# Binding the matmul order of the first four Strassen units of an FFN, with one more split product

## The chip, the cores and the metric

The kernel runs on one core of a Trainium2 chip. The metric is device time of one execution in microseconds (us), lower is better. TensorE (PE in the profile) multiplies matrices, with PEld its weight loads; VectorE (DVE) and ScalarE (ACT) do elementwise work; GpSimd (POOL) and SyncE (SP) issue most of the transfers.

## The reference

A decoder block in float32 for 512 tokens of width 1024: two token mixers and then a SwiGLU channel mixer (FFN) of inner width 2816. The change lies in the FFN alone:

```python
    x = x + rms_norm(mixed @ w_out[l], norm_mix_post[l])
    h = rms_norm(x, norm_ffn_pre[l])
    f = (jax.nn.silu(h @ w_ffn_gate[l]) * (h @ w_ffn_up[l])) @ w_ffn_down[l]
    x = x + rms_norm(f, norm_ffn_post[l])
```

## The kernel before

**Precision.** Each float32 factor is split into a high part (a cast to the 32-bit matmul type) and a low part (the value minus the cast). A product is three matmuls, `three(o, w, x, start, stop)`: high weight by high input (L243), high weight by low input (L248), low weight by high input (L249). The weight's cast is made by ScalarE (L1427, L1447), its low half by VectorE (L1454) or by a transfer that GpSimd issues and that adds the weight onto the negated cast (L1429, L1431).

**FFN units.** The gate and up weights come in 22 row tiles `n` of 128 output columns. Tiles 0 to 2 are plain products. From tile `N0` = 3 on, `unit(n)` makes gate and up tile together by the Strassen-Winograd scheme: the 2 x 2 blocks are (gate, up) times (first, second half of the width 1024) on the weights' side, and (first, second half of the width) times (two halves of 256 tokens) on the inputs' side. Seven products, in the program's order a11, s2, s3, s1, a12, a22, s4, stand in place of eight. `product(o, a, b, first)` makes one: four steps of 128 in depth, each one call of `three` on 256 columns, so 12 matmuls.

**Weight forms.** a11, a12 and a22 are splits of the raw weights (`prep_g`, `prep_u`), in buffers named whi/wlo, w_g3h/w_g3l and w_uu. s1 to s4 are sums and differences made by VectorE (`sums_s` L1462 and L1463, `sums_t` L1468 and L1469), then split by `split_pair`, s1 with s2 and s3 with s4, into one of three slots by turns (d_two twice, c_two). `prep_st(n + 1)` is written behind `unit(n)`. The input forms (hT_hi/hT_lo, x4, x5, x) are made once ahead of the first unit by `x_forms` (L1490, L1491), the last two of them inside it, by `between`.

**PSUM.** The first unit has its four results r1, rb, r2, ra in two banks of `ps_tp`; the others have a bank for each, by turns `ps_sc`/`ps_mm` and `ps_tp`/`ps_acc`. VectorE adds the results (L1536: us, wk), ScalarE applies silu to each token half (L1545), VectorE multiplies (L1546). `plain_out` (L1400 to L1404) finishes the three plain tiles and is written between the first units.

**What sets the order.** The program is traced in Python, and a scheduler then orders each engine's instructions: of those that are ready in its plan, the one that was traced first goes next. So TensorE's order is not the written one where a written product's operands are late in the plan. `tc.issue_after(ins)` puts the instructions of its block behind `ins` in the queue of that instruction's engine, with no wait of its own.

**Cut products.** `restart()` sets a flag; the next call of `three` on 256 columns then makes its second matmul in two pieces of 128 columns. Before the change the flag is set, among other places, ahead of the first unit's a11 and ahead of s1 of the fourth unit (n == N0 + 3).

Of the kernel before, what the change touches and what calls it, by code (L numbers as in the profile page):

```python
# [150 lines left out]
def hybrid_block_kernel(ctx: ExitStack, tc: tile.TileContext, I, outT):  # L151
# [15 lines left out]
    def bank(tag):  # L167
        return psum.tile([128, 512], F32, tag=tag, bufs=2, name="ps_" + tag)
# [45 lines left out]
    for key in with_gla + with_cmp + with_att + late:  # L214
        kind, n = key
# [20 lines left out]
    def restart():  # L236
        fresh[0] = True

    def three(o, w, x, start, stop):

        (wh, wl), (xh, xl) = w, x
        n = o.shape[1]
        pe.matmul(o, wh, xh, start=start, stop=False, skip_group_check=True)  # L243
        cut = [slice(0, 128), slice(128, 256)] if fresh[0] and n == 256 else [slice(0, n)]
        if n == 256:
            fresh[0] = False
        for c in cut:
            pe.matmul(o[:, c], wh, xl[:, c], start=False, stop=False, skip_group_check=True)  # L248
        return pe.matmul(o, wl, xh, start=False, stop=stop, skip_group_check=True)  # L249
# [62 lines left out]
    for k in range(KD):  # L312
# [10 lines left out]
        last = act.activation(out=hu[:, k, :], in_=xt, func=AF.Copy, scale=g_pre[:, k:k + 1])  # L323
# [202 lines left out]
    stk = {}  # L526
# [20 lines left out]
    for g in range(3):  # L547
        pss = [bank(t) for t in tags[g]]
        for c in range(4):
# [6 lines left out]
            for i, kk, m in turns:  # L556
# [6 lines left out]
                o = pss[i][:, 0:TG]  # L563
# [272 lines left out]
    def plain_pair(q, u):  # L836

        return (tile_pieces(q, {0: [lambda: eload(u)] if u == 0 else [],
                                2: [lambda: esums(u), lambda: eform(u, "a22", True)],
                                3: [lambda: eform(u, "a11"), lambda: eform(u, "s2"), lambda: esum_s1(u)]})  # L840
                + tile_pieces(q, {0: [lambda: eform(u, "a12", True)], 1: [lambda: esum_s4(u), lambda: eform(u, "s4")],
                                  3: [lambda: eform(u, "s3"), lambda: eform(u, "s1"), lambda: eload(u + 1)]}))
# [5 lines left out]
    def pair(u, then=(), at=(1, 3)):  # L848

        def one(i):  # L850
            eproduct(u, i)
            if then and i in at:
                st.after = out_of[u, a] if (a := USE[i][0]) in ("s1", "s4") else None
                ahead(then[at.index(i)])
            if not then:
                next_forms(u, i)
        return [lambda i=i: one(i) for i in range(7)]
# [3 lines left out]
    first = plain_pair(qa, 0)  # L861
# [6 lines left out]
    first = pair(0, (15, 16), (3, 5))  # L868
# [356 lines left out]
    q = Pieces(with_att)  # L1225
# [157 lines left out]
    def fraw(n):  # L1383
        if n >= 2 * KH + 4:
            return slot(n - 2 * KH)
        if n < 2 * KH:
            i, tag = n % KH, "a%d" if n < KH else "hh%d"
        else:
            i, tag = n - 2 * KH, "hl%d"
        tag = tag % (i // 2)  # L1390
        if tag not in room:
            room[tag] = quad(tag, F32, "f" + tag)
        return room[tag][:, i % 2, :]
# [13 lines left out]
    N0 = NPLAIN  # L1407
# [113 lines left out]
    def unit(n, between=None):  # L1521
        if n == N0:
            p1, p2 = bank("tp"), bank("tp")
            r1, rb, r2, ra = p1[:, 0:256], p1[:, 256:512], p2[:, 0:256], p2[:, 256:512]
        else:
            pair = ("sc", "mm") if (n - N0) % 2 else ("tp", "acc")
            r1, r2, rb, ra = [bank(tag)[:, 0:256] for tag in pair for _ in range(2)]

        def product(o, a, b, first):
            (ah_, al_), (bh_, bl_) = forms.pop((n, a)), XF[b]  # L1530
            for q in range(4):
                c = slice(q * 128, (q + 1) * 128)
                three(o, (ah_[:, c], al_[:, c]), (bh_[q], bl_[q]), first and q == 0, q == 3)

        def add(out, ps, b):
            dve.tensor_tensor(out=out, in0=ps, in1=b, op=OP.add)  # L1536

        us = ffn.tile([128, 2, 256], F32, tag="us", bufs=2, name="us")
        wk = ffn.tile([128, 3, 256], F32, tag="wk", bufs=2, name="wk")
        sl = ffn.tile([128, S], F32, tag="sl", bufs=2, name="sl")  # L1540
        fr[n] = fraw(n)

        def half_out(e, g):
            t = halves[e]
            act.activation(out=sl[:, t], in_=g, func=AF.Silu)  # L1545
            dve.tensor_tensor(out=fr[n][:, t], in0=sl[:, t], in1=wk[:, 1 + e, :], op=OP.mult)  # L1546

        if n == N0:
            restart()
        product(r1, "a11", "b11", True)  # L1550
        act.copy(us[:, 0, :], r1)
        product(r2, "s2", "t2", True)
        add(us[:, 0, :], r2, us[:, 0, :])
        product(rb, "s3", "t3", n > N0)
        add(us[:, 1, :], rb, us[:, 0, :])
        end = between() if between else None
        if n == N0 + 3:
            restart()
        product(ra, "s1", "t1", n > N0)
        add(wk[:, 2, :], ra, us[:, 1, :])  # L1560
        product(r1, "a12", "b21", False)
        product(rb, "a22", "t4", False)
        add(wk[:, 1, :], rb, us[:, 0, :])
        product(ra, "s4", "b22", False)
        add(wk[:, 0, :], ra, us[:, 0, :])
        half_out(0, r1)
        half_out(1, wk[:, 0, :])
        return end
# [56 lines left out]
    first = (bank("sc"), bank("sc"))  # L1625
# [51 lines left out]
    for n in range(N0, KF):  # L1677
        if n + 2 < KF:
            load(n + 2, "w_gate")
            load(n + 2, "w_up")  # L1680
        last = unit(n, rest_of_forms if n == N0 else None)
        if n == N0:
            end = last
            plain_out(1, *second)
        if n == N0 + 1:
            plain_out(2, *third)
        if n + 1 < KF:
            prep_st(n + 1, end)
        if n + 2 < KF:
            prep_g(n + 2)  # L1690
            prep_u(n + 2)
        if 2 * KH <= n < 2 * KH + 4:
            down_t3(n - 2 * KH)
# [294 lines left out]
```

## Time and profile before

| | |
|---|---|
| median of 3 runs | 842.55 us (841.9 to 842.9) |
| profiled execution, time | 843.94 us |
| profiled execution, span from the first to the last instruction | 841.7 us |
| TensorE busy | 827.2 us (98%) |
| VectorE busy | 632.5 us (75%) |
| ScalarE busy | 523.6 us (62%) |
| first matmul of the first Strassen unit | 531.93 us |
| first matmul of the fifth unit | 572.43 us |

Times in rows of the profile are microseconds from the span's start. A row of the timeline has its start, its duration, the engine, the line of the kernel, the operation, the tile written and those read, their shape, the count, and in square brackets the idle time ahead of it with what ended it. A row of a table of stretches has the stretch, its length, the busy time and number of instructions of each engine, the granted TensorE clock (1.00 is full speed), the share of the DMA engines and the rate in GB/s. Durations of matmuls overlap: their rate is read from the distance between starts.

### The profile page before, as it was taken

The page shows a single profiled execution, that of the slowest core. Times are in us where ns is not written, and L with a number is a line of the kernel's source. Part 1 is how long each engine was busy: PE and PEld are TensorE (multiplying, and loading weights), DVE is VectorE, ACT ScalarE, POOL GpSimd, SP SyncE. Part 2 cuts the span into 40 slices and gives each one's busy share as a digit, 9 for nine tenths or more (in the row PEclk, how much of TensorE's full clock was granted, in tenths as well). Part 3 has the DMA queues.
Part 4 walks back from the last instruction along what each step waited for, and adds up shares of the span by engine and source line. Part 5 has one row for each costly group of instructions (what it writes and reads, how often), then busy time and mean ns, then how long its engine had stood idle before and what let it go on. Part 6 is the DMA issues. An engine that isn't in the chain of part 4 may idle for free.

```text
span 841.7 us, 14734 instructions
## 1 busy us (share of the span) xinstructions
PE 827.2 (98%) x5593; PEld 754.4 (90%) x5593; DVE 632.5 (75%) x1209; ACT 523.6 (62%) x963; POOL 144.9 (17%) x174
## 2 busy tenths in 40 slices
PE   9999999999999999999999999999999999999995
PEld 8998899999788888888878999999999999889995
DVE  7766887873376778877667468998888778939886
ACT  6557767764364888888645577766665566535441
POOL 0101022221040000010000364111121110001353
PEclk9999999999999999999999999999999999999997
DMA  8434366863241544445227759779888883225333
GB/s 290 108 101 113 97 124 132 172 134 92 75 158 51 116 111 109 118 102 123 63 65 251 246 151 234 147 208 224 205 179 194 199 192 86 81 86 176 88 102 101
DMA packets 41239, 117.86 MB, mean 140 GB/s; under 512 B 4716, under 2 KB 7036, under 8 KB 41040
## 3 DMA queue, kind: packets, MB, share of 16 engines
q1 hardware_dynamic: 27952, 82.49, 31.8%
q0 software_dynamic: 12496, 33.88, 21.8%
q8 instruction: 44, 0.72, 0.3%
q10 hardware_dynamic: 720, 0.54, 0.2%
q14 instruction: 27, 0.22, 0.1%
HBM read 102.21 MB, written 4.19 MB: 126 GB/s over the span
## 4 chain that ended last, share of the span: by engine, by line
PE 75%; DVE 5%; ACT 3%; issue 2%; DMA 2%; POOL 0%; DVEq 0%; ACTq 0%; SPq 0%; POOLq 0%
PE ps_mm L243 12%; PE ps_mm L249 12%; PE ps_mm L248 12%; PE ps_sc L243 5%; PE ps_sc L249 5%; PE ps_sc L248 5%; PE ps_acc L243 4%; PE ps_acc L248 3%; PE ps_acc L249 3%; PE ps_tp L243 2%; PE ps_tp L249 2%; PE ps_tp L248 2%; PE ps_tp L1128 2%; PE ps_acc L1143 1%; PE ps_sc L1078 1%
## 5 line engine op out<-in xcount | busy, mean ns | idle before, releaser
L78 ACT CAST whi<-wraw 128x1024 fp32r<-128x1024 f32 (+2 forms) x62 | 60.1, 973 | 66.4 <-PE ps_mm L248 22.2
L243 PE MATMUL ps_mm<-hT_hi,whi 128*128 128x512 f32 (+1 forms) x260 | 100.4, 386 | 0.2 <-ACT whi L78 0.2
L249 PE MATMUL ps_mm<-hT_hi,wlo 128*128 128x512 f32 (+1 forms) x260 | 97.0, 374 | 0.0
L248 PE MATMUL ps_mm<-hT_lo,whi 128*128 128x512 f32 (+1 forms) x259 | 96.6, 374 | 0.0
L85 DVE TENSOR_TENSOR wlo<-wraw,whi 128x1024 fp32r<-128x1024 f32 (+2 forms) x47 | 51.4, 1095 | 27.5 <-ACT whi L78 25.1
L249 PEld LDWEIGHTS ps_mm<-hT_hi,wlo 128*128 128x128 f32 x260 | 48.8, 188 | 9.3 <-DVE wlo L85 0.3
L243 PEld LDWEIGHTS ps_mm<-hT_hi,whi 128*128 128x128 f32 x260 | 48.9, 188 | 9.0 <-ACT whi L78 0.9
L248 PEld LDWEIGHTS ps_mm<-hT_lo,whi 128*128 128x128 f32 x259 | 48.7, 188 | 7.0
L1447 ACT CAST d_two<-s 128x1024 fp32r<-128x1024 f32 x26 | 27.0, 1044 | 30.5 <-PE ps_mm L249 15.0
L274 DVE TENSOR_TENSOR pl<-ps_tp,ph 128x512 fp32r<-128x512 f32 (+1 forms) x64 | 31.1, 489 | 14.9 <-ACT ph L273 14.2
L1088 ACT ACTIVATE p<-p,mx 128x512 f32<-128x512 f32 (+1 forms) x64 | 35.9, 561 | 9.2 <-DVE mx L1086 8.6
L1454 DVE TENSOR_TENSOR d_two<-s,d_two 128x1024 fp32r<-128x1024 f32 x25 | 30.6, 1223 | 11.2 <-ACT d_two L1447 11.0
L82 POOL DMA_DIRECT2D wlo<-wraw x15 | 12.8, 851 | 149.1 <-ACT wlo L81 101.2
L1086 DVE CUSTOM_DVE_ANT_0 p<-ps_sc,causal 128x512 f32<-128x512 f32 (+1 forms) x64 | 30.2, 486 | 9.9 <-PE ps_sc L1079 9.5
L273 ACT CAST ph<-ps_tp 128x512 fp32r<-128x512 f32 (+1 forms) x64 | 26.5, 416 | 4.3 <-PE ps_tp L1128 3.9
L1128 PE MATMUL ps_tp<-ident,p 128*128 128x128 f32 x160 | 27.9, 272 | 0.0
L1128 PEld LDWEIGHTS ps_tp<-ident,p 128*128 128x128 f32 x160 | 20.7, 140 | 7.2 <-ACT pc L1017 0.4
L1820 POOL TENSOR_TENSOR y<-y,us 128x256 f32<-128x256 f32 x12 | 14.4, 1224 | 70.7 <-DVE us L1817 70.7
L1431 POOL DMA_DIRECT2D wlo<-in_w_gate x13 | 11.5, 887 | 76.9 <-ACT wlo L1429 76.8
L1447 ACT CAST c_two<-s 128x1024 fp32r<-128x1024 f32 x12 | 12.5, 1043 | 18.7 <-PE ps_acc L249 9.6
L243 PE MATMUL ps_mm<-hT_hi,d_two 128*128 128x256 f32 x80 | 22.5, 281 | 0.0
L249 PE MATMUL ps_mm<-hT_hi,d_two 128*128 128x256 f32 x80 | 22.3, 279 | 0.0
(820 smaller groups left out, 3226.0 us busy)
## 6 DMA issues: line engine op xcount, KB each, us to landing
wraw<-in_w_t SPq DMA_DIRECT2D x36, 512.0 KB, 3.9
wraw<-in_w_gate SPq DMA_DIRECT2D x21, 512.0 KB, 4.5
rw<-in_w_up SPq DMA_DIRECT2D x19, 512.0 KB, 8.3
wlo<-wraw POOLq DMA_DIRECT2D x15, 512.0 KB, 4.5
wlo<-in_w_gate POOLq DMA_DIRECT2D x13, 512.0 KB, 7.8
w_uu<-in_w_up POOLq DMA_DIRECT2D x19, 256.0 KB, 8.7
wraw<-in_w_tok SPq DMA_DIRECT2D x11, 440.0 KB, 3.5
wraw<-in_w_proj SPq DMA_DIRECT2D x8, 512.0 KB, 3.6
```

The costliest lines, as they stand in the source:

```text
L78: self.cast = self.nc.scalar.copy(hi[:, :cols], raw[:, :cols])
L85: self.nc.vector.tensor_tensor(out=lo[:, :cols], in0=raw[:, :cols], in1=hi[:, :cols].bitcast(F32), op=OP.subtract)
L243: pe.matmul(o, wh, xh, start=start, stop=False, skip_group_check=True)
L248: pe.matmul(o[:, c], wh, xl[:, c], start=False, stop=False, skip_group_check=True)
L249: return pe.matmul(o, wl, xh, start=False, stop=stop, skip_group_check=True)
L273: act.copy(hi, src)
L274: dve.tensor_tensor(out=lo, in0=src, in1=hi.bitcast(F32), op=OP.subtract)
L1086: dve.tensor_tensor_reduce(out=o, in0=s, in1=causal[:, S - n:S], scale=-1.0, scalar=-NEG, op0=OP.add, op1=OP.min, accum_out=mx[:, i:i + 1])
L1088: act.activation(out=o, in_=o, func=AF.Exp, scale=-1.0, bias=mx[:, i:i + 1], accum_out=z[:, i:i + 1])
L1128: pe.transpose(tp[:, i * 128:(i + 1) * 128], p[:, OFF[i] + k * 128:OFF[i] + (k + 1) * 128], ident)
L1447: act.copy(hi, t)
L1454: dve.tensor_tensor(out=lo, in0=t, in1=hi.bitcast(F32), op=OP.subtract)
```

## The change

Each product of the units N0 to N0 + 3 has its first call of `three` queued on TensorE behind the last matmul of the product traced before it; the other three calls follow by accumulating into the same PSUM region. The first product of all has none ahead of it. Units from N0 + 4 on are traced without this edge. The flag for a cut product is also set ahead of s1 in unit N0. No other instruction is added or taken away.

```diff
         def product(o, a, b, first):
             (ah_, al_), (bh_, bl_) = forms.pop((n, a)), XF[b]
+            last = stk.get("unit") if n < N0 + 4 else None
             for q in range(4):
                 c = slice(q * 128, (q + 1) * 128)
-                three(o, (ah_[:, c], al_[:, c]), (bh_[q], bl_[q]), first and q == 0, q == 3)
+                with tc.issue_after(last.ins) if last and q == 0 else nullcontext():
+                    stk["unit"] = three(o, (ah_[:, c], al_[:, c]), (bh_[q], bl_[q]), first and q == 0, q == 3)
...
         end = between() if between else None
-        if n == N0 + 3:
+        if n in (N0, N0 + 3):
             restart()
         product(ra, "s1", "t1", n > N0)
```

## The prediction

> **What bounds the kernel now.** I read the page's busy shares and the chain that ended last first, then the busy time of each engine in stretches around the first Strassen units, then the timelines of TensorE (PE), VectorE (DVE) and ScalarE (ACT) inside them.
>
> ```profile
> PE 827.2 (98%) x5593; PEld 754.4 (90%) x5593; DVE 632.5 (75%) x1209; ACT 523.6 (62%) x963; POOL 144.9 (17%) x174
> PE 75%; DVE 5%; ACT 3%; issue 2%; DMA 2%; POOL 0%; DVEq 0%; ACTq 0%; SPq 0%; POOLq 0%
> ```
>
> TensorE is busy 98% of the span and carries most of the chain: an idle TensorE is paid in full, and only its order, its stalls and its rate can move the time. The next rows are stretches (length; busy time and count of PE, PEld, DVE, ACT, POOL; granted clock; DMA share; GB/s), the last two for PE alone.
>
> ```profile
> 531.93:543.40 11.47, 11.47 (x98) 11.42 (x97) 11.16 (x17) 7.83 (x13) 1.15 (x2) 1.00 0.51 99
> 543.40:557.05 13.65, 13.62 (x113) 13.27 (x112) 13.59 (x23) 9.20 (x15) 1.49 (x3) 1.00 0.81 211
> 572.43:715.23 142.80, 142.80 (x1262) 142.80 (x1261) 117.22 (x207) 89.40 (x141) 23.10 (x27) 1.00 0.78 184
> 531.93:572.43 40.50, 40.47 (x339) 1.00 0.74 168
> 572.43:581.95 9.52, 9.52 (x86) 1.00 0.94 250
> ```
>
> Call the first four units U0 to U3. They run from 531.93 to 572.43 us: 4 x 7 products x 12 = 336 matmuls of 256 columns (two cut into halves), 40.50 us. The unit behind them takes 9.52 us for 84, so 113.3 ns each; at that rate 336 would take 38.1 us. So 2.3 us is the most that a better order could win here. But in the first two stretches DVE is busy 11.16 of 11.47 and 13.59 of 13.65 us: at this place DVE has no slack, while later it has (117.22 of 142.80). DVE still works off the forms of the activations, and the low halves of the weight forms queue behind them. TensorE has no gap only because it takes products of other units meanwhile.
>
> **The change part by part: the rate.** Start times of the first and the thirteenth matmul of runs of 12, and a cut product:
>
> ```profile
> 552.81 0.28 PE L243 MATMUL ps_mm<-x5h,w_uu 128*128 128x256 f32 x1
> 554.22 0.28 PE L243 MATMUL ps_mm<-x,d_two 128*128 128x256 f32 x1
> 566.97 0.33 PE L248 MATMUL ps_mm<-hT_lo,d_two 128*128 128x128 f32 x2
> 567.14 0.34 PE L249 MATMUL ps_mm<-hT_hi,d_two 128*128 128x256 f32 x1
> 569.71 0.28 PE L243 MATMUL ps_mm<-x5h,w_uu 128*128 128x256 f32 x1
> 571.07 0.28 PE L243 MATMUL ps_mm<-x,d_two 128*128 128x256 f32 x1
> ```
>
> At 552.81 twelve matmuls take 1.41 us (117.5 ns each); behind the cut at 566.97 they take 1.36 us (113.3 ns). So there are two rates, 4.2 ns apart at equal clock, and a cut brings the fast one. The added cut in U0 costs 0.17 us for the pair in place of 0.12: +0.05 us. It could win up to 4.2 ns for each of the some 190 matmuls up to the cut in U3, 0.8 us, if nothing knocks the stream back.
>
> **The binding inside U0.**
>
> ```profile
> 533.97 1.22 DVE L1454 TENSOR_TENSOR d_two<-s,d_two 128x1024 fp32r<-128x1024 f32 x1
> 535.01 0.28 PE L243 MATMUL ps_sc<-hT_hi,w_g3h 128*128 128x256 f32 x1
> 535.24 0.38 PE L249 MATMUL ps_tp<-hT_hi,d_two 128*128 128x256 f32 x1
> 536.24 0.41 DVE L1536 TENSOR_TENSOR us<-ps_tp,us 128x256 f32<-128x256 f32 x1
> 536.49 0.28 PE L249 MATMUL ps_sc<-hT_hi,w_g3l 128*128 128x256 f32 x1
> 536.72 0.37 PE L243 MATMUL ps_tp<-hT_hi,d_two 128*128 128x256 f32 x1
> ```
>
> s3 needs the low half that DVE finishes at 535.19; at 535.01 TensorE takes two matmuls of U1's a11 instead (into ps_sc) and returns at 535.24. s1 writes the bank that the add at 536.24 still reads, until 536.65; again two matmuls of U1 (536.49) fill the wait, and s1 starts at 536.72. Bound, these two holes of 0.23 us each stay empty: s1 still starts at 536.72, 48 matmuls with one cut at 113.3 to 117.5 ns end U0 at 542.2 to 542.4, and U1's a11, now whole, ends at about 543.7.
>
> **U1's s2.**
>
> ```profile
> 541.71 0.68 DVE L1463 TENSOR_TENSOR s<-s,wraw 128x512 f32<-128x512 f32 x1
> 542.98 1.04 ACT L1447 CAST c_two<-s 128x1024 fp32r<-128x1024 f32 x1
> 543.40 0.28 PE L243 MATMUL ps_tp<-hT_hi,whi 128*128 128x256 f32 x1
> 544.06 1.22 DVE L1454 TENSOR_TENSOR c_two<-s,c_two 128x1024 fp32r<-128x1024 f32 x1
> 544.07 0.39 PE L243 MATMUL ps_sc<-hT_hi,c_two 128*128 128x256 f32 x1
> 545.48 0.28 PE L249 MATMUL ps_sc<-hT_hi,c_two 128*128 128x256 f32 x1
> ```
>
> ACT casts s2's high half until 544.02, DVE makes the low half until 545.28. Before, 13 matmuls of U2's a11 (543.40, into ps_tp) and U1's a12 cover this. Bound, TensorE stands from 543.7 to 544.07, issues the two matmuls on the high half, and stands from 544.3 to 545.3: 1.4 us. Ten more end s2 at 546.5.
>
> **U1's s3.**
>
> ```profile
> 546.13 0.68 DVE L1468 TENSOR_TENSOR s<-wraw,rw 128x512 f32<-128x512 f32 x1
> 546.73 0.68 DVE L1469 TENSOR_TENSOR s<-wraw,s 128x512 f32<-128x512 f32 x1
> 547.56 0.39 ACT L1545 ACTIVATE sl<-ps_sc 128x256 f32<-128x256 f32 x1 [2.44 <-PE ps_sc L249]
> 547.85 1.04 ACT L1447 CAST d_two<-s 128x1024 fp32r<-128x1024 f32 x1
> 548.92 1.23 DVE L1454 TENSOR_TENSOR d_two<-s,d_two 128x1024 fp32r<-128x1024 f32 x1
> 548.94 0.39 PE L243 MATMUL ps_mm<-hT_hi,d_two 128*128 128x256 f32 x1
> 550.57 0.28 PE L249 MATMUL ps_mm<-hT_hi,d_two 128*128 128x256 f32 x1
> ```
>
> The sums end at 547.41, the cast at 548.89, the low half at 550.15. DVE runs from 544.06 to here without a break, and what it does is traced earlier in the program than these sums, so they have no reason to move up. Earliest: the silu at 547.56 waits for a12, which now comes later, so the cast can start at 547.45 and end at 548.5, and the low half follows at once, 1.23 us: 549.7. Latest: 550.15 as now. I take the late end, because DVE takes up other ready work while the cast runs. TensorE stands from 546.5 to 548.5 or 548.9, issues two matmuls and stands again: 3.4 us lost in U1's s3.
>
> **From there on.**
>
> ```profile
> 555.93 0.86 POOL L1431 DMA_DIRECT2D w_g3l<-in_w_gate  x1 [11.97 <-PE ps_mm L249]
> 556.18 1.22 DVE L1454 TENSOR_TENSOR c_two<-s,c_two 128x1024 fp32r<-128x1024 f32 x1
> 564.30 1.22 DVE L1454 TENSOR_TENSOR d_two<-s,d_two 128x1024 fp32r<-128x1024 f32 x1
> w_g3l<-in_w_gate POOLq DMA_DIRECT2D x3, 512.0 KB, 8.6
> ```
>
> Behind the third matmul of s3, at 550.2, 226 matmuls are left up to U3's end: 25.6 us at 113.3 ns, and 0.06 us for U3's cut, which stays. TensorE reaches U2's s3 near 559.5 and U3's near 569; the low halves were there at 557.4 and 565.5, so no further stall. The loads that wait for a buffer of U1's or U2's a12 (SP's, and POOL's low halves such as the one at 555.93, 8.6 us to land) go out up to 7 us later; that one lands near 572, and U4 that uses it starts near 576, which is cover of about 4 us. Adds, silus and half outputs shift with their products, into a stretch where DVE and ACT then have slack.
>
> U3 ends at 550.2 + 25.7 = 575.9 against 572.43: +3.4 us. With the early low half it is +3.0; with all of the 200 matmuls up to 20 behind U3's cut at the slow rate +0.8 on top, so +4.3. The row at 552.81 shows the slow rate behind such disturbances; I put in a fifth of the 0.8. Sum: +3.5 us. Everything later is bound by TensorE (142.80 of 142.80) and moves along. On the profiled execution, 843.94 us with 841.7 of span and 2.2 around it, this gives 847.4; it stands 1.4 above the median of the runs, 842.55, on which I predict **846.0 us**.
>
> [...]
>
> ```profile
> 829.65 0.28 PE L249 MATMUL ps_sc<-db,wlo 128*128 128x256 f32 x1
> 832.66 0.58 PE L294 MATMUL ps_tp<-ident,rs 128*128 128x128 f32 x1 [1.15 <-POOL rs L288]
> 832.00:833.00 1.00, 0.34 (x1) 0.35 (x2) 0.76 (x3) 0.00 (x0) 0.60 (x1) 0.82 0.07 24
> 833.00:834.00 1.00, 0.88 (x4) 0.58 (x3) 0.09 (x1) 0.00 (x0) 0.00 (x0) 0.50 0.75 247
> ```
>
> At the tail the granted clock falls to 0.50: a mean of 0.82 between 832 and 833 puts the fall at 832.64, 3.0 us after the start of the last dense matmul, with a few one-column matmuls between. My stall around s3 is 3.7 us with two dense matmuls in it. If the clock falls there and takes as long to return, 3 us at half speed cost 1.5 us: 847.5. [...]
>
> **The rivals.** (1) The clock falls in the stall, as above: 847.5 us. For it, the tail; against it, the two matmuls between. (2) Faster: DVE and ACT, arranged anew around the bound order, make U1's forms first. If s34's low half (548.92 now) is there when TensorE gets to s3, near 545, only U0's holes of 0.46 us stay and the rest runs at 113.3 ns: 2.3 - 0.5 - 0.05 = 1.8 us less, 840.8. It decides where that low half ends before about 546; against it, DVE's queue from 531.93 on is full of work traced earlier. (3) Half of that: the low half ends near 547.5, and the time is within 0.2% of before, about 843.5. (4) The order hardly changes, so that the change doesn't do what it says: 842.5. Against it, the rows at 535.01, 536.49 and 543.40 are of other units, which the binding forbids. (5) U3's cut does not bring the fast rate: 4.2 ns for the 1262 matmuls up to 715.23, 5.3 us more, 851. Against it, the row at 569.71.
>
> **How the numbers follow.** My forecast 0.55 (844.9 to 847.0); rival 1 0.23 (to 848.6); rival 2 0.09; rivals 3 and 4 together 0.10; rival 5 0.03. Measurement can tell 0.2%, 1.7 us, from no change. Slower: 0.55 + 0.23 + 0.03 and a little of rival 3, 0.82; same 0.09; faster 0.09. The range from 843.3 to 848.6 leaves out rival 2, rival 5 and the lower part of 3 and 4, about 2 in 10.
>
> **What would show it.** In the changed kernel's timeline each step has its mark: no ps_sc matmul before U0's end; TensorE idle in front of U1's s2 and s3, released by ACT's cast and DVE's low half (L1447, L1454); those low halves ending near 545.3 and 549.7 to 550.2; runs of 12 in 1.36 us from U3's cut on; U3's end near 575.9; a granted clock of 1.00 in the stall, or below if rival 1 holds. The prediction is wrong if U1's low halves come some 3 us earlier, or if something besides the four units fills the gaps.

## The result, and the profile after

| | before | after |
|---|---|---|
| median of 6 executions each | 842.87 us (841.9 to 844.43) | 848.37 us (846.2 to 850.3) |
| profiled execution, time | 843.94 us | 849.46 us |
| span | 841.7 us | 847.2 us |

The ratio is 1.0056, with a 95% interval of 1.0043 to 1.007: slower, by 5.5 us. The prediction had said slower with 846.0 us and a range of 843.3 to 848.6. Its direction and its places were right; some 2 us were missing, and these are what the experiments had to find.

The busy shares and the chain that ended last, after:

```profile
PE 829.6 (98%) x5594; PEld 756.2 (89%) x5594; DVE 633.1 (75%) x1209; ACT 524.2 (62%) x963; POOL 142.4 (17%) x174
PE 80%; DVE 8%; ACT 7%; issue 3%; DMA 1%; POOL 1%; SPq 0%; ACTq 0%; DVEq 0%; POOLq 0%
```

One PE instruction more is the cut. VectorE and ScalarE now carry 8% and 7% of the chain in place of 5% and 3%. The page can't say more; the stretches of the first four units can (columns as before: stretch, length, PE, PEld, DVE, ACT, POOL, granted clock, DMA share, GB/s):

```profile
531.24:577.60 46.36, 42.73 (x341) 41.52 (x340) 41.36 (x67) 27.65 (x42) 5.11 (x6) 0.96 0.72 168
531.24:541.89 10.65, 10.55 (x87) 10.15 (x86) 10.65 (x16) 6.94 (x11) 0.39 (x1) 1.00 0.59 114
541.89:553.64 11.75, 8.22 (x50) 7.42 (x49) 10.05 (x16) 4.74 (x8) 1.31 (x2) 0.85 0.76 185
553.64:577.60 23.96, 23.96 (x208) 23.96 (x207) 20.66 (x36) 15.97 (x24) 3.41 (x4) 1.00 0.75 184
```

The four units take 46.36 us in place of 40.50, +5.86. They start 0.7 us earlier, and from U3's end to the end of the span it is 269.6 us against 269.3, so next to nothing behind them counts. In U0 (second row) and from U1's a12 to U3's end (last row) TensorE hardly stands: it is busy 10.55 of 10.65 and 23.96 of 23.96 us. The loss sits in the third row, from U1's start to its a12, so in U1's a11, s2, s3 and s1: PE busy 8.22 of 11.75 us, and a granted clock of 0.85.

Some rows of TensorE's timeline in U1, s2 first, then s3, the wait in brackets; and below it what VectorE and ScalarE did:

```profile
545.41 0.39 PE L249 MATMUL ps_sc<-hT_hi,c_two 128*128 128x256 f32 x1 [1.41 <-DVE c_two L1454]
547.69 0.39 PE L243 MATMUL ps_mm<-hT_hi,d_two 128*128 128x256 f32 x1 [0.87 <-ACT d_two L1447]
549.41 0.38 PE L249 MATMUL ps_mm<-hT_hi,d_two 128*128 128x256 f32 x1 [1.22 <-DVE d_two L1454]
549.99 0.35 PE L243 MATMUL ps_mm<-hT_hi,d_two 128*128 128x256 f32 x1
550.36 0.42 PE L249 MATMUL ps_mm<-hT_hi,d_two 128*128 128x256 f32 x1
550.58 0.41 PE L243 MATMUL ps_mm<-hT_hi,d_two 128*128 128x256 f32 x1
...
553.35 0.34 PE L248 MATMUL ps_mm<-hT_lo,c_two 128*128 128x256 f32 x1
```

```profile
544.14 1.22 DVE L1454 TENSOR_TENSOR c_two<-s,c_two 128x1024 fp32r<-128x1024 f32 x1
545.88 0.68 DVE L1469 TENSOR_TENSOR s<-wraw,s 128x512 f32<-128x512 f32 x1
546.59 1.04 ACT L1447 CAST d_two<-s 128x1024 fp32r<-128x1024 f32 x1 [2.05 <-DVE s L1469]
```

The three waits are the predicted ones: s2's third matmul for the low half that VectorE starts at 544.14, s3's first for a cast that itself waited for VectorE's sum of 545.88, s3's third for that form's low half. None of another unit's matmuls stands between them. Behind 549.99 the third thing shows: neighbouring matmuls 0.21 us apart, where they were 0.12 apart just ahead, for 3.4 us. The granted clock says why (rows for PE alone: stretch, length, PE, granted clock, DMA share, GB/s):

```profile
546.64:550.05 3.41, 1.33 (x9) 1.00 0.99 314
550.05:553.46 3.41, 3.41 (x18) 0.50 0.45 135
553.46:556.88 3.42, 3.42 (x31) 1.00 0.70 229
```

From 550.05 to 553.46, 3.41 us, the clock was at half speed; 1.00 and 0.50 are the only values in the profiles of the two kernels. The last is the rate at clock 1.00, by the starts of the first and thirteenth matmul of U1's a22 and of U3's a12 behind its cut:

```profile
555.05 0.28 PE L243 MATMUL ps_mm<-x5h,w_uu 128*128 128x256 f32 x1
556.47 0.28 PE L243 MATMUL ps_mm<-x,d_two 128*128 128x256 f32 x1
...
573.51 0.28 PE L243 MATMUL ps_sc<-x4h,whi 128*128 128x256 f32 x1
574.88 0.28 PE L243 MATMUL ps_mm<-x5h,w_uu 128*128 128x256 f32 x1
```

1.42 us against 1.37: the slow rate, and it held from U0's cut to U3's, but for a few matmuls of U1's s2 (0.57 us for five from 545.98 on).

So three terms are in question: the waits, the fall of the clock, the slow rate. The theory on trial: the binding alone causes the waits, because VectorE is late and nothing may fill in; the other two come on top of the prediction's sum, by about 1.5 and 0.8 us. (The kernel before ran most of this stretch at the slow rate too, so the 0.8 us are a gain that the forecast counted on and that did not come.) Its rivals: the added cut does part of the harm; the order itself costs something even when nothing is late; the waits cost more than their length for another reason than the clock.

### The profile page after: what moved, and what is told of

Its sections match the earlier page's. It is cut to its first block, busy times and chain, and to the rows that moved or that the text cites. A ratio compares the mean times of both kernels' runs of the same rounds, so it can differ in the third digit from the quotient of the medians.

```text
span 847.2 us, 14747 instructions
## 1 busy us (share of the span) xinstructions
PE 829.6 (98%) x5594; PEld 756.2 (89%) x5594; DVE 633.1 (75%) x1209; ACT 524.2 (62%) x963; POOL 142.4 (17%) x174
## 4 chain that ended last, share of the span: by engine, by line
PE 80%; DVE 8%; ACT 7%; issue 3%; DMA 1%; POOL 1%; SPq 0%; ACTq 0%; DVEq 0%; POOLq 0%
PE ps_mm L243 11%; PE ps_mm L249 11%; PE ps_mm L248 11%; PE ps_sc L243 5%; PE ps_sc L248 5%; PE ps_sc L249 5%; PE ps_acc L243 3%; PE ps_acc L249 3%; PE ps_acc L248 3%; PE ps_tp L565 2%; PE ps_tp L249 2%; PE ps_tp L243 2%; PE ps_tp L248 2%; PE ps_sc L565 2%; PE ps_tp L1128 1%
## 5 line engine op out<-in xcount | busy, mean ns | idle before, releaser
L1822 POOL TENSOR_TENSOR y<-y,us 128x256 f32<-128x256 f32 x12 | 12.7, 1080 | 71.1 <-DMA wraw<-in_w_down 69.3
```

## The experiments

In each, the stretch is that from U0's first matmul to U3's last (40.50 us before, 46.36 after), from one profiled execution.

**Which half of the change: e1_cut_only and e2_bind_only.** e1 is the kernel before with this edit, e2 the change without it.

```diff
-        if n == N0 + 3:
+        if n in (N0, N0 + 3):
             restart()
```

> Only the added cut in U0's s1, no binding; the matmul order is that of before. Theory (the binding makes TensorE wait for U1's low halves, and the clock falls in the gap): within 0.2% of before, 842 to 844 us, no idle TensorE in U1, clock 1.00 there, U0's start to U3's end 40 to 40.6 us. Rival (the extra cut disturbs the stream and is what costs): as slow as the change, 847 us or more, U0 to U3 near 46 us.

> Only the binding of the products of U0 to U3, without the added cut. Theory: as slow as the change, ratio to before 1.004 to 1.007, TensorE idle for 3 to 3.5 us ahead of and inside U1's s2 and s3, U0's start to U3's end 45 to 46.5 us, a fall of the granted clock to 0.50 behind s3 for about 3.4 us. Rival (the cut costs): within 0.2% of before.

Measured: the cut alone 844.32 us, ratio 1.0015 (1.0005 to 1.0026); the binding alone 848.46, ratio 1.0071 (1.0051 to 1.0092). Their stretches and, for the binding, TensorE's waits at s3 and the clock around them:

```profile
531.43:572.28 40.85, 40.06 (x340) 39.27 (x339) 39.40 (x65) 27.55 (x42) 5.12 (x6) 1.00 0.73 174
```

```profile
531.52:577.95 46.43, 42.63 (x340) 41.35 (x339) 41.41 (x67) 28.11 (x42) 5.12 (x6) 0.93 0.70 167
548.07 0.58 PE L243 MATMUL ps_mm<-hT_hi,d_two 128*128 128x256 f32 x1 [1.80 <-ACT d_two L1447]
549.78 0.58 PE L249 MATMUL ps_mm<-hT_hi,d_two 128*128 128x256 f32 x1 [0.92 <-DVE d_two L1454]
547.50:555.00 7.50, 6.01 (x27) 0.54 0.66 216
```

The binding is the whole loss. Two details matter later. Without the cut, U0 from a12 on and U2 and U3 run at 113.3 ns; so the fast rate came without a cut, where the change with a cut had the slow one. And the clock was at half for 2 x 0.46 x 7.5 = 6.9 us, twice as long as after. The cut alone is no gain either: its plan came out a little different, with a wait of 0.47 us in U2's s3, and far behind the units one of 1.39 us at 773.45, where before's profile has one of 0.26.

**What the fall of the clock costs: e3_fill.** The change, with spare matmuls in U1's holes: 12 ahead of the wait in s2, 8 ahead of s3, 11 between its second and third matmul. They open an accumulation of their own in the banks of s2 and s3, so that a part of these two products is lost: e3, e9 and e10 leave out a part of the computation, and only their times are of use.

```diff
+    FILL = {"s2": (0, 12), "s3": (8, 11)}
...
+        last = fill(side, ahead, last)
+        with tc.issue_after(last.ins):
+            pe.matmul(o, wh, xh, start=True, stop=False, skip_group_check=True)
+            last = pe.matmul(o, wh, xl, start=False, stop=False, skip_group_check=True)
+        last = fill(side, inside, last)
+        with tc.issue_after(last.ins):
+            pe.matmul(o, wl, xh, start=False, stop=False, skip_group_check=True)
...
```

> The change, with 31 spare matmuls put into the gaps of U1 (12 inside s2, 8 ahead of s3 and 11 inside it), into PSUM columns that nothing reads; the forms come no sooner, so the waits for them stay, but TensorE is busy in them. Theory (the clock falls because of the gap): granted clock 1.00 from U1 on, no matmul at 213 ns, time 1.4 to 1.8 us under the change's, U0's start to U3's end 44 to 45 us. Rival (the fall has another cause, or its price is hidden by other waits): clock falls as before or the stretch stays at 46 us.

```profile
531.33:576.15 44.82, 44.64 (x371) 43.55 (x370) 41.27 (x67) 27.66 (x42) 5.12 (x6) 1.00 0.71 172
```

Measured 847.14 us, ratio 1.0052 (1.0031 to 1.0073). The holes are full (44.64 of 44.82 us), the clock stays at 1.00, s3's third matmul still comes at about 549.5, and the slow rate is there as in the change. The stretch is 1.54 us shorter: that is the price of 3.4 us at half speed, as rival 1 of the prediction had it (1.5). In the medians, 847.14 against 848.37 us, the intervals of the two ratios overlap.

**Where the waits come from: e4_free_a11.** The change, with the a11 of U1 to U3 out of the chain of edges.

```diff
-                with tc.issue_after(last.ins) if last and q == 0 else nullcontext():
-                    stk["unit"] = three(o, (ah_[:, c], al_[:, c]), (bh_[q], bl_[q]), first and q == 0, q == 3)
+                with tc.issue_after(last.ins) if last and q == 0 and a != "a11" else nullcontext():
+                    mark = three(o, (ah_[:, c], al_[:, c]), (bh_[q], bl_[q]), first and q == 0, q == 3)
+            if a != "a11" or n == N0:
+                stk["unit"] = mark
```

> The change, but a11 of U1, U2 and U3 is left unbound, so that 36 of the 336 matmuls may go into the gaps of U0 and U1; the rest keeps the bound order. Theory (only the cover of U1's gaps is missing): the waits inside s2 and s3 are filled, about 0.9 us ahead of s3 is left, no fall of the clock, U0's start to U3's end 40.5 to 42 us, ratio to before 0.999 to 1.002. Rival (strict order itself or bank conflicts cost): stays above 1.004.

```profile
531.35:573.34 41.99, 40.13 (x341) 39.10 (x340) 40.93 (x67) 29.02 (x43) 5.12 (x6) 1.00 0.75 175
```

Measured 844.44 us, ratio 1.0019 (1.0009 to 1.0028). Three products that need only raw weights, free to move, give back 4.4 of the 5.9 us, clock and rate included: the waits shrink (0.49 us at s2's third, 0.84 at s3's first, none at its third), and the clock does not fall. The holes of the change are the fillers that it forbade.

**Is it VectorE's order: e5_bind_forms_first, e6_forms_first, e12_bind_forms_twice.** `prep_st(n + 1)` is written ahead of `plain_out`, so that the sums and low halves of U1 (e12: of U1 and U2) are traced ahead of the plain tiles' finish; e5 and e12 on the change, e6 on the kernel before. The edit of e5 and e6 (e12 does the same once more ahead of `plain_out(2, *third)`):

```diff
         if n == N0:
             end = last
+            prep_st(n + 1, end)
             plain_out(1, *second)
         if n == N0 + 1:
             plain_out(2, *third)
-        if n + 1 < KF:
+        if N0 < n and n + 1 < KF:
             prep_st(n + 1, end)
```

> The change, with U1's weight forms traced ahead of the second plain tile's output, so that three VectorE instructions of 0.6 us each come behind s34's sums instead of ahead of them. Theory (what TensorE waits for is VectorE's queue): the low half for s3 ends about 1.5 us earlier against U0's start than in the change (18.1 us there), the waits in U1 shrink from 3.5 us to 2 us or less, no fall of the clock, U0 to U3 42.5 to 44 us, ratio to before 1.001 to 1.004. Rival (the waits come from ScalarE's casts or from PSUM banks): waits of 3 us or more, U0 to U3 over 45 us.

> The kernel before with only U1's weight forms traced ahead of the second plain tile's output; no binding, no added cut. Theory: TensorE was kept busy in U1 before by other units' products, so earlier forms change little but need fewer of them: U0 to U3 39.5 to 40.7 us, ratio to before 0.998 to 1.001. Rival (the pulled-forward products cost time by themselves, up to the 2.3 us over the fast rate): U0 to U3 near 38.5 us, ratio 0.998 or less.

> The change, with U1's and U2's forms both traced ahead of the plain tiles' finish (with U1's alone the stretch was 43.90 us and the one wait left was 1.6 us at U2's s3). Theory (a bound order costs only what VectorE is late): U2's s3 waits no longer than 0.3 us, stretch 42.0 to 42.8 us, ratio 1.001 to 1.003. Rival (VectorE has no slack until U3, so the lateness moves on to U2's s4 or U3's s2): stretch 43.5 to 44.5 us, ratio 1.003 to 1.006.

The stretch and TensorE's longest waits in it for e5, then the stretch and the waits in U3 for e6, then the stretch, its one long wait and the clock behind it for e12:

```profile
531.60:575.50 43.90, 40.58 (x340) 39.39 (x339) 41.33 (x67) 27.60 (x42) 5.12 (x6) 1.00 0.73 176
545.70 0.39 PE L249 MATMUL ps_sc<-hT_hi,c_two 128*128 128x256 f32 x1 [1.41 <-DVE c_two L1454]
...
558.75 0.38 PE L249 MATMUL ps_acc<-hT_hi,c_two 128*128 128x256 f32 x1 [1.41 <-DVE c_two L1454]
```

```profile
531.79:575.18 43.39, 41.07 (x339) 39.69 (x338) 38.42 (x63) 26.99 (x41) 5.12 (x6) 1.00 0.71 164
567.79 0.39 PE L249 MATMUL ps_mm<-hT_hi,d_two 128*128 128x256 f32 x1 [0.50 <-DVE d_two L1454]
573.66 0.39 PE L243 MATMUL ps_mm<-x,d_two 128*128 128x256 f32 x1 [0.24 <-DVE wk L1536]
```

```profile
530.51:574.19 43.68, 41.98 (x341) 41.19 (x339) 41.04 (x67) 27.65 (x42) 5.11 (x6) 0.96 0.73 177
544.60 0.39 PE L249 MATMUL ps_sc<-hT_hi,c_two 128*128 128x256 f32 x1 [1.41 <-DVE c_two L1454]
544.50:548.50 4.00, 3.90 (x20) 0.57 1.00 219
```

e5, 846.83 us, 1.0039 (1.0026 to 1.0052): s3 of U1 waits no more, and a wait of 1.41 us, as long as the one left at U1's s2, appears at U2's s3; VectorE's lateness has moved by a unit. (The column for VectorE is full in both kernels' U0; there is no slack to take it from.) e12, 845.67 us, 1.0035 (1.0015 to 1.0055): U2's wait is gone as well and nothing later takes its place, as the theory said. But the stretch is 43.68 and not 42.0 to 42.8: the clock fell for 2 x 0.43 x 4 = 3.4 us behind s2's one wait, and behind that the rate was the slow one up to U3's cut.

e6 is a miss: 847.86 us, 1.006 (1.0033 to 1.0087), where a stretch of 39.5 to 40.7 us was expected. With no edge to hold it, the planned order of the kernel before came out quite different, with waits of 0.63 and 0.76 us in U2 and of 0.50 and 0.24 us in U3. The latter stands behind U3's cut at 569.17, and the fast rate that the cut had brought was lost: the next 1262 matmuls behind U3 took 148.87 us against 143.27, 5.6 us more, and from U3's end to the end it is 274.0 us against 269.3. That is the prediction's rival 5 (5.3 us) in another kernel. The times of e6 spread from 844.3 to 854.4 us, and the profiled execution, 851.55, is one of the slower; how often the fast rate is lost is not known.

**Sums on another engine: e7_pool_forms, e8_bind_pool_forms.** U1's four sums go to GpSimd and lose their place behind the input forms; e7 on the kernel before, e8 on the change.

```diff
...
-        s12 = sums_s(g, u, after)
+        on = pool if n == N0 + 1 else dve
+        s12 = sums_s(g, u, after if on is dve else None, on)
```

> The kernel before, with U1's four sums for s1 to s4 made by GpSimd instead of VectorE and without their place behind the input forms; no binding, no added cut. Theory: VectorE's queue is shorter by 2.4 us and U1's forms are there on time, so TensorE goes through U1 nearly in the written order: no matmul of U2 or U3 in U1, waits under 1 us, U0 to U3 38.5 to 40 us, ratio to before 0.997 to 1.000. Rival (GpSimd's sums are slower and late, or hold up its transfers): waits in U1 or U2, U0 to U3 above 41 us.

> The change with U1's four sums made by GpSimd. Theory (late forms, not the order, cost the time): with the forms on time the bound order costs only U0's holes of about 0.5 us; no fall of the clock, waits in U1 under 1 us, U0 to U3 38.7 to 40.5 us, ratio to before 0.997 to 1.001, so the change's loss is gone. Rival (the strict order itself costs): ratio above 1.004 again.

Both missed: 846.72 us, 1.0038 (1.0023 to 1.0053), stretch 44.64 us, and 846.46 us, 1.0031 (1.0018 to 1.0044), stretch 43.97 us. e7's timeline has where the time went: three rows of VectorE, the GpSimd sums beside them, and TensorE's wait (L1492 and L1537 here are L1491 and L1536 of the kernel before).

```profile
535.37 1.47 DVE L1404 TENSOR_TENSOR fa<-fa,fu 128x512 f32<-128x512 f32 x1
537.10 1.96 DVE L1492 TENSOR_TENSOR x5l<-nb,x5h 128x1024 fp32r<-128x1024 f32 x1
538.98 3.45 DVE L1492 TENSOR_TENSOR x<-nb,x 128x512 fp32r<-128x512 f32 x2
531.80 4.49 POOL L1462 TENSOR_TENSOR s<-rw 128x512 f32<-128x512 f32 x1 [3.74 <-DVE hT_lo L1492]
...
540.18 1.71 POOL L1469 TENSOR_TENSOR s<-wraw,s 128x512 f32<-128x512 f32 x1
542.91 0.55 PE L243 MATMUL ps_tp<-x,d_two 128*128 128x256 f32 x1 [2.27 <-DVE wk L1537]
```

The same three rows took 0.68, 1.21 and 1.28 us before: 3.7 us more in sum, while VectorE's adds with one operand in PSUM kept their 0.41 us. It was not so for all: beside GpSimd's first sum, which took 4.49 us where the others took 1.61 to 2.28, three VectorE instructions with two SBUF inputs kept their 1.22 us. Why the two engines were slow beside each other was not shown. So s4 of U0 waits 2.27 us, and the clock falls at the end of that wait, at 542.83.

e8 has the same wait in U0 (2.28 us), and with the half clock behind it this gives VectorE time. So e8 answers another question all the same:

```profile
547.76:575.12 27.36, 27.36 (x243) 1.00 0.81 200
```

From U1's s2 (547.76) to U3's end (575.12), its bound products run without one wait and, but for the first, at 113.3 ns: 27.36 us for 240 matmuls, of which 27.19 at 113.3 ns and 0.05 for U3's cut. The order by itself costs nothing where the forms are there in time.

**Which holes the clock fell behind, and whether a cut sets the rate: e9_fill_s2, e10_fill_s3in, e11_cut_u1.** e9 fills only s2's hole, e10 only the one between s3's second and third matmul (both edits on e3); e11 is the change with one more cut product, U1's s1, just behind the waits. In this order:

```diff
-    FILL = {"s2": (0, 12), "s3": (8, 11)}
+    FILL = {"s2": (0, 12)}
...
-    FILL = {"s2": (0, 12), "s3": (8, 11)}
+    FILL = {"s3": (0, 11)}
...
-        if n in (N0, N0 + 3):
+        if n in (N0, N0 + 1, N0 + 3):
```

> The change with 12 spare matmuls ahead of U1's s2's third matmul's wait only (spare matmuls open their own accumulation in that bank, so a part of the computation is changed); the holes around s3 stay empty. Theory (the holes around s3 alone throttle the clock): TensorE still waits some 2.1 us around two matmuls of s3, the granted clock falls to 0.50 near 550 for 3 us or more, and the stretch from U0's start to U3's end is 46.0 to 46.8 us. Rival (the idle time of s2 and s3 counts together, some 3.5 us in 5.4): with s2 filled the clock stays at 1.00, and the stretch is 44.6 to 45.2 us.

> The change with 11 spare matmuls between the second and the third matmul of U1's s3 only (they open their own accumulation in that bank, so a part of the computation is changed); 1.4 us ahead of s2's third and 0.9 us ahead of s3's first stay empty. Theory (it takes about 2 us of idle time broken by two matmuls at most): no fall of the clock, stretch 44.6 to 45.1 us. Rival (the sum of the holes from s2 on counts, and 2.3 us of it are still there): the clock falls near 549 to 550, stretch 46 to 46.8 us.

> The change with one more cut product, U1's s1, behind the stalls. Theory of the prediction (a cut brings the fast rate): from U1's s1 on 113.3 ns in place of 117.5 for about 150 matmuls, stretch 0.5 to 0.65 us shorter than the change's 46.36, with the same waits and fall of the clock: 45.7 to 45.9 us. Rival (the rate is drawn anew at a disturbance, and a cut doesn't decide it): 117.5 ns again behind the cut and 46.3 to 46.5 us, or 113.3 ns already ahead of it.

The stretches of e9 and e10, e10's wait and clock, and e11's stretch with its waits at s3 and its clock; the two rows of the clock, last in each fence, are for PE alone:

```profile
532.12:576.08 43.96, 41.54 (x353) 40.35 (x352) 41.22 (x67) 27.58 (x42) 5.12 (x6) 1.00 0.74 176
```

```profile
530.47:575.08 44.61, 42.89 (x351) 41.67 (x350) 41.30 (x67) 27.65 (x42) 5.11 (x6) 0.96 0.71 174
544.54 0.42 PE L249 MATMUL ps_sc<-hT_hi,c_two 128*128 128x256 f32 x1 [1.41 <-DVE c_two L1454]
541.34:544.75 3.41, 1.80 (x13) 1.00 0.76 113
544.75:548.16 3.41, 3.41 (x16) 0.50 1.04 260
```

```profile
532.08:576.15 44.07, 40.28 (x342) 39.09 (x340) 41.11 (x67) 27.58 (x42) 5.11 (x6) 1.00 0.73 175
548.43 0.39 PE L243 MATMUL ps_mm<-hT_hi,d_two 128*128 128x256 f32 x1 [0.86 <-ACT d_two L1447]
550.15 0.39 PE L249 MATMUL ps_mm<-hT_hi,d_two 128*128 128x256 f32 x1 [1.22 <-DVE d_two L1454]
545.71:549.12 3.41, 1.92 (x12) 1.00 1.00 221
549.12:552.54 3.42, 2.39 (x20) 1.00 0.64 240
```

Medians 848.01, 847.61 and 848.48 us; ratios 1.006 (1.004 to 1.008), 1.0066 (1.0042 to 1.009) and 1.0065 (1.0039 to 1.0091). None came wholly as one of its two theories had it, and e11 tells most. Its waits are those of the change (1.41, 0.86 and 1.22 us), and its clock stayed at 1.00; its rate was 113.3 ns from U0 on, ahead of the new cut already, as its rival had put it, so that the cut had nothing to bring. In e10 the clock did fall, at 544.8, behind s2's wait alone, where the change had kept its clock behind the same wait. So the same holes bring the fall in one execution and not in another; e9's clock of 1.00 then says nothing of s2's part, only its 2.07 us of waits at s3 are once more without a fall.

How the holes lie, as measured: in the change the clock was at half for 3.41 us, in e10 and e12 for 3.4, in e7 and e8 for about as long, in e2 for 6.9. In the 3.41 us ahead of each of these six falls TensorE was idle for 1.61 us or more: 1.61 in e10 and e12, 1.99 in e2, 2.08 in the change, 2.18 in e7 and 2.28 in e8. The last two rows of e10 here, and the first two of the change's clock further up, are such a stretch and the half clock behind it; idle time is the length less PE's busy time. But about as much idle time did not always bring a fall. e11, whose waits are the change's, was idle for 2.07 of the 3.41 us up to 550.15, e9 for 2.06 of those up to 550.20 and e5 for 1.60 of those up to 545.70, and the clock of each stayed at 1.00. Cut at 549.12, as in its rows, e11 has 1.49 and 1.03 us of idle time. So the idle time did not decide by itself. That its place in time does is a guess; no run tested it.

In e2 the first 3.4 us at half had about 1.1 us of idle time, and as long a stretch at half followed. In the tail, where TensorE runs matmuls of one column, before's clock fell at 832.64 behind 3.41 us with 1.13 us of idle time (2.28 us busy).

The mean granted clock that is on record for every execution bears on those that were not profiled; by an estimate, 3.41 us at half in a span of some 845 us takes 0.002 off it. The 54 executions of the kernel before that ran beside the experiments lie at 0.994 to 0.996 and e3's five, with the holes filled, at 0.995 and 0.996; the change's six lie at 0.992 to 0.996 and e2's four at 0.991 to 0.994.

## Why the prediction was right, and where it was short

- **The places and the waits: right.** U1's s2 waits 1.41 us, where 1.4 was put; s3 waits 2.1 us and its third matmul comes at 549.41, which is 550.10 in before's frame (U0 starts 0.69 us earlier), where 550.2 was taken as the late end. U2 and U3 have no wait. The late transfers did no harm: U4 starts without one. What lies between was not as put. s2's low half started at 544.14, no sooner than before (544.06) though the units started 0.69 us earlier, so s2 ended about 0.85 us later, in before's frame, than put; and the stop around s3, its two matmuls included, was 2.75 us (546.66 to 549.41) where 3.7 were put. VectorE's order had changed too, against "they have no reason to move up": the first sum for s3 (L1468) ran at 542.88 in place of 546.13. That s3's low half, on which the sum rests, still came at the late end is in part luck.
- **The sum of the mechanism: right.** e11 is the change with neither the fall nor the slow rate, and one cut more. Its stretch is 44.07 us, +3.57 over before, +3.5 without the extra cut. The prediction had +3.4 for that case.
- **The slow rate: mis-sized.** "I put in a fifth of the 0.8" was the term. In the profiled execution the whole of it was paid: e3, with the clock at 1.00 and the slow rate, takes 44.82 us, 0.75 more than e11, 0.8 beside e11's extra cut.
- **"A cut brings the fast rate": fell as a rule.** It came without the cut (e2), it didn't come with it (the change, e3), and it was lost behind U3's cut (e6). What the profiles show is less: the rate changed at a cut (117.5 to 113.3 ns at U3's in the change), at a wait (113.3 to 117.5 at the 1.41 us of U2's s3 in e5) and at a wait with a fall of the clock (the same in e12), and in these three it stayed as it was between such places, by the starts of every twelfth matmul. Behind U3's cut it was 113.3 ns in each of the bound kernels.
- **The clock: rival 1 happened.** The price of 1.5 us was right (1.54 by e3), its chance of 0.23 too low: among seven profiles with about 1.9 us of holes or more near U1 (after, e2, e5, e9, e10, e11, e12) it fell in four, and in e7 and e8 it fell behind U0's hole. The forecast of 846.0 put nothing for the clock in gaps broken by two matmuls, and no run shows that as a rule. What the runs showed: it fell behind waits of 0.87 and 1.22 us in the change, in one of 1.80 in e2, behind one of 1.41 in e10 and e12, and with waits of 0.85 or 0.86 and 1.22 in e9 and e11 it stayed at 1.00.
- **The account.** In the prediction's terms, 3.5 us of waits at the fast rate, 0.8 of slow rate and 1.54 of clock make +5.8; measured +5.86 in the stretch. Against the kernel before the split is another, as that ran at the slow rate too. By the distances between starts, less 113.3 ns for each, before's stretch has 1.2 us in longer distances and 1.0 in the rate; the change's has 5.5, 0.9 and 1.6 at half clock. So the waits cost 4.3 us, the clock 1.6, and the rate nothing. Less the 0.7 us by which the units start earlier, and with 0.3 behind them, that is the 5.5 of the times.
- **Rivals 2, 3 and 4: refuted.** The low half of s3's form was not made earlier (it started 16.9 us behind U0's start, 17.0 before), and the order did change. VectorE's queue is the reason: moving U1's forms up (e5) moved the wait to U2.

No version here beat the kernel before; the nearest bound one, e4, is 0.2% slower. How often an execution of the changed kernel has the fall and the slow rate stays open: its times, 846.2 to 850.3 us, spread 4 us, and only one of them was profiled. By the mean granted clock the executions at 0.993 and 0.992, under all of before's, had a fall, and the one at 0.996 had none; that is an estimate from the 0.002. What sets the rate is open too.

## What to carry to other kernels

An order of the scheduler that looks untidy may be cover: before fixing it, ask for each product pulled forward what it stands in for, and read when the operands of the product behind it are ready. Where the engine that makes them is full, a bound order turns its lateness into idle time, and moving one unit's forms up handed the wait to the next unit (e5); with two units' moved up it did not come back (e12). Price the holes with what follows them: two waits of 0.87 and 1.22 us cost another 1.54 us here by the clock (the change against e3), and holes like them cost nothing by the clock in e9 and e11.

## What the runs showed that I had not expected

- The granted clock fell behind waits of 0.87 and 1.22 us (the change), or one of 1.41 and a short one of 0.20 (e10, e12), and stayed at half for 3.41 us, in e2 for 6.9; waits of 1.41, 0.86 and 1.22 us left it at 1.00 in e11.
- Dense matmuls of 256 columns ran 113.3 or about 117.8 ns apart at a clock of 1.00 here, and what decides which was not found; over 1262 matmuls behind U3 that was 5.6 us (e6), as much as this change cost.
- With four GpSimd sums beside it, three rows of VectorE's instructions with two SBUF inputs took 6.9 us in place of 3.2 (e7), 3.7 us more; moving the sums had taken 2.7 us (four at 0.68) off it.
